# Staging of the output gate z in its own half-sized pool, and a pool of its own for what the attention lays over it, in a hybrid two-layer decoder

## The chip, the cores and the metric

The kernel runs on one core of one Trainium2 chip. The metric is the device time of one execution in microseconds (us); the figure for a kernel is the median over its runs. The engines are TensorE (PE; its weight loads are shown apart as PEld), VectorE (DVE), ScalarE (ACT), GpSimd (POOL) and SyncE (SP), which issues most of the DMAs. Each engine works through its own queue in order. SBUF is the memory on the core, PSUM the accumulators that TensorE writes.

## What is computed

Two layers, each of the form h += RMSNorm(mixer(RMSNorm(h))), then h += sigmoid(h W_g) * (p W_p). The mixer of layer 0 is retention and mLSTM heads, that of layer 1 sixteen attention heads in four groups and an S5 branch. The change lies in layer 1, in the attention and its gate z:

```python
proj = (u @ w_in).astype(F32)
nq, kc, vc, ks, vs, kw, vw, ng, nz, su, sz = _split(proj, CD_SIZES)
y_nsa = nsa(nq, kc, vc, ks, vs, kw, vw, ng, ...)   # compressed, selected and sliding-window branches
y_nsa = y_nsa * jax.nn.silu(nz)
mix = jnp.concatenate([y_nsa, y_s5], -1).astype(u.dtype)
return mix @ w_out
```

Inside `nsa` each token attends to 63 compressed blocks, to 4 selected blocks of 64 keys, and to a window of 512 keys; the three results are added with gates of their own. Everything is float32.

## The kernel before

All matrix products but a few are made of three reduced-precision products: a matrix x is kept as a rounded part `hi` and a remainder `lo`, and hi·hi, hi·lo and lo·hi are added up in PSUM. ACT writes `hi`, DVE (or POOL) the remainder.

The program is written as one long function, `body`. It doesn't fix the order of the instructions: a scheduler with a time model of its own puts them in order on each engine when the program is built, and waits are set from the places that tiles take in SBUF. A tile whose place overlaps an older tile waits until that tile is done with; the scheduler knows of this wait and orders the queues by it. With `reuse_waits="tile"` such a wait is set tile by tile.

Layer 1 first makes its projections (`nsa_projections`, a generator that is advanced one piece at a time, called `gen`). Each piece is a product `pj` into one PSUM bank, ACT and DVE work on it into a staging tile, and a DMA to DRAM. The pieces are 16 of the queries (staging `qst`), 8 of keys (`kst`), 8 of values (`vst`, L1111), and 16 of the gate z (`zt`, L1133): tanh on ACT (L1134), a product on DVE (L1135), a store to `zD` on SP (L1136). All staging tiles have the tag `st` in the pool `pd[0]`; a tile of z uses half of a place of 4,096 bytes per partition. The pool is `pd` first, and `pd2` from L1255 on, three places, on the right-hand side of SBUF, just below the layer's normalised input `vh`, `vl`.

The attention works in 32 units, one group of four heads by one tile of 128 queries (`units`). For a unit, `head` (L1348) makes the compressed branch: scores `cs`, `scc` (L1367 to L1375), the mask `mg` of the selected blocks, and `cp`. `scores` (L1412) makes the other two branches, window (b=1) and selection (b=0): products `sc`, a pass of DVE per piece that adds the mask and finds the maximum (L1425), and the exponential on ACT (L1428) into `pr`; `scale` (L1433) divides by the sum. `values` (L1482) then takes 128 keys at a time: four turns of `pr` on TensorE (`pt`, L1487), the split into `pthh` on ACT (L1478) and `pthl` on DVE (L1479), two products `av`. At the end of the unit `oc` and `ob` collect the result, and it is multiplied by the unit's z, `zn`, which SP loads from `zD` (L1627).

The last z pieces run while the attention begins: the loop at L1451 advances `gen` and puts the heads of units 0 and 1 and both `probabilities` of unit 0 among the last of them. Then `ph3` closes (L1460), the places of `vh` and `vl` come free, and pool `n2` opens (L1469). Its tiles lie on the left, from 144,960 bytes up: `zn` (three of 1,024), `pthh` (three of 2,048, from 148,032), `pthl` (three of 2,048, from 154,176 to 160,320), `oc`, `ob`. `pd2` has 151,520 to 163,808. So the last two `pthh`, all `pthl`, `oc` and `ob` lie on staging places, and `zn` and the first `pthh` don't.

Beside the attention runs `filler`, which advances the S5 branch and the output projection by a credit per unit: its first piece loads `w_glu` (`raw`, split to `whi`, `wlo`, L159 and L160 on ACT and POOL) and two tiles of `y5D` (L1528) that ACT splits to `fhi` (L1499).

Of the kernel before, what the change touches and what calls it, by code (L numbers as in the profile page):

```python
# [17 lines left out]
FT = mybir.dt.float32  # L18
# [79 lines left out]
def body(tc, A, out, dbg=None):  # L98
# [24 lines left out]
    def const_load(p, name, bufs=1):  # L123
        o, n = LAY[name]
        x = p.tile([128, n], FT, name="c_" + name, tag="c_" + name, bufs=bufs)
        nc.scalar.dma_start(x, A["consts"][:, o:o + n])
        return x
# [40 lines left out]
    def chunk(w, segs, nkt=8, kt0=0, gain=None, pack=True):  # L168

        if pack and sum(b for _, b in segs) <= 256:  # L170
            x = [load_w(w, segs, kt0 + 4 * k, 4, gain) for k in range(nkt // 4)]
            return [tuple(y[:, 2 * j:2 * j + 2] for y in c) for c in x for j in range(2)]
        return [load_w(w, segs, kt0 + 2 * k, 2, gain) for k in range(nkt // 2)]
# [668 lines left out]
    class Ext:  # L842
# [5 lines left out]
        def next(self):  # L848
            self.n += 1
            return self.p[self.pat[(self.n - 1) % len(self.pat)]]  # L850
# [228 lines left out]
    def nsa_projections(pd):  # L1079
# [47 lines left out]
        for c in range(4):  # L1127
            ck = chunk(W1, [(2608 + 256 * c, 256)])
            for half in range(2):
                for m in range(2):  # L1130
                    ps = pz[0][0].tile([128, 512], FT, name="pj", tag=pz[0][1])
                    proj_col(ps, uT, half, ck, m * 128)
                    zt = pd[0].tile([128, 2, 512], FT, name="zt", tag="st")[:, 0]  # L1133
                    s.activation(zt, ps, AF.Tanh, scale=0.5)  # L1134
                    v.scalar_tensor_tensor(zt, zt, 1.0, ps, op0=OP.add, op1=OP.mult)  # L1135
                    nc.sync.dma_start(zD[2 * c + m, :, half * 512:(half + 1) * 512], zt)  # L1136
                    yield
# [19 lines left out]
    with ExitStack() as e:  # L1157
        ed = ExitStack()
        pd = [ed.enter_context(tc.tile_pool(name="pd", bufs=3, reuse_waits="tile"))]
# [4 lines left out]
        gen = nsa_projections(pd)  # L1164
# [87 lines left out]
        ed.close()  # L1252
        n1 = ctx.enter_context(tc.tile_pool(name="n1", bufs=1, reuse_waits="tile"))
        nq = ctx.enter_context(tc.tile_pool(name="nq", bufs=3, reuse_waits="tile"))
        pd[0] = e.enter_context(tc.tile_pool(name="pd2", bufs=3, side="right", reuse_waits="tile"))  # L1255
        scaus, wmask = const_load(n1, "scaus"), const_load(n1, "wmask")
        kmask, force = const_load(n1, "kmask"), const_load(n1, "force")
        late = const_load(n1, "late")
# [10 lines left out]
        for kv in range(2):  # L1269
# [55 lines left out]
            else:  # L1325
# [3 lines left out]
                s.activation(vcT[:63, :, 0:64], p3_, AF.Copy)  # L1329
                v.tensor_tensor(vcT[:63, :, 64:128], p3_, vcT[:63, :, 0:64].bitcast(FT), op=OP.subtract)  # L1330
                s.activation(vcT[64:127], vcT[:63].bitcast(FT), AF.Copy)
        for _ in range(9):
            next(gen)
        ec.close()
        px_.close()
        nh = ctx.enter_context(tc.tile_pool(name="nh", bufs=2, reuse_waits="tile"))
# [130 lines left out]
    ext1 = Ext(dict(x=xf), "xxwxwwxw")  # L1467
    with ExitStack() as e:
        n2 = e.enter_context(tc.tile_pool(name="n2", bufs=2, reuse_waits="tile"))  # L1469
        pT = e.enter_context(tc.tile_pool(name="pT", bufs=3, space=PSUM, reuse_waits="tile"))  # L1470
        pV = e.enter_context(tc.tile_pool(name="pV", bufs=1, space=PSUM, reuse_waits="tile"))
        pF = e.enter_context(tc.tile_pool(name="pF", bufs=1, space=PSUM, reuse_waits="tile"))
# [150 lines left out]
        FOFF = -1000  # L1623
        for n, (gg, i) in enumerate(units):
            rows = slice(i * 128, (i + 1) * 128)
            zt = n2.tile([128, 2, 128], FT, name="zn", tag="zn", bufs=3)
            nc.sync.dma_start(zt, zD[2 * gg:2 * gg + 2, :, rows].rearrange("a p k -> p a k"))  # L1627
            if n % 8 == 2 and gg < 3:
                KV[gg + 1] = group(gg + 1)
# [33 lines left out]
            step(gg, ns / 2)  # L1663

            a4 = acc.rearrange("p (a b k) -> p a b k", a=2, b=2)
            oc = n2.tile([128, 2, 128], FT, name="oc", tag="oc", bufs=1)
            ob = n2.tile([128, 2, 128], FT, name="ob", tag="ob", bufs=1)
            lo_, up = slice(0, 64), slice(64, 128)
            for b, here, there in ((0, lo_, up), (1, up, lo_)):
                s.activation(oc[here], a4[there, :, b], AF.Copy)  # L1670
# [74 lines left out]
```

## Time and profile before

| | us |
|---|---|
| median of 3 runs | 2356.01 |
| lowest, highest run | 2354.99, 2358.60 |
| profiled execution | 2355.67 |
| its span, first to last instruction | 2353.6 |
| TensorE busy in the span | 2273.9 |
| DVE, ACT, POOL busy | 1469.6, 1073.4, 487.9 |

The profile gives for each instruction its start, its length, how long its engine had been idle before it, and what ended that idle time. A window row gives the busy time of each engine in a stretch and the TensorE clock that the throttle granted, 1.00 being 2.4 GHz and 0.50 being 1.2. Matmuls overlap, so the time that one costs is read from a run of them, not from its own length.

### The profile page before, as it was taken

To read this page: it belongs to the slowest core of one execution; us is meant where nothing else is said; L and a number is where in the kernel's file an instruction comes from. 1 tells how busy PE (TensorE), PEld (TensorE's weight loads), DVE (VectorE), ACT (ScalarE), POOL (GpSimd) and SP (SyncE) were. 2 spreads that over 40 slices of the span, in tenths; PEclk is the share of its full clock that TensorE was granted. 3 is DMA by queue.
4 is the path that set the end of the run, shared out by engine and by line. 5 is a ranking of instruction groups with operands and counts; after the bars stand their busy time and mean duration, and the time that the engine had idled before them with its cause. 6 is when DMAs were issued, how large, how long until landed. Compare 5 with 4: busy or idle time off the path is not lost.

```text
span 2353.6 us, 34485 instructions
## 1 busy us (share of the span) xinstructions
PE 2273.9 (97%) x11974; PEld 1904.1 (81%) x11974; DVE 1469.6 (62%) x3893; ACT 1073.4 (46%) x2345; POOL 487.9 (21%) x585
## 2 busy tenths in 40 slices
PE   7999999999999999999999999989999989999898
PEld 6888889787888788888888889768988878878677
DVE  6777746755654424444287353368887898888943
ACT  6223323433332432233232233167787786778821
POOL 0222200000000000200000010034354244566720
PEclk9999999999999999999999999989999999999999
DMA  6423312020221645424367524442363443355643
GB/s 160 92 79 107 97 50 72 19 72 27 81 72 37 210 148 206 136 90 136 112 193 246 142 75 131 120 124 77 95 180 107 123 127 97 103 172 155 199 165 111
DMA packets 266696, 279.27 MB, mean 119 GB/s; under 512 B 54384, under 2 KB 200408, under 8 KB 266490
## 3 DMA queue, kind: packets, MB, share of 16 engines
q1 hardware_dynamic: 254810, 244.48, 34.3%
q10 hardware_dynamic: 8096, 23.67, 3.0%
q0 software_dynamic: 3616, 8.92, 1.4%
q8 instruction: 95, 1.56, 0.3%
q14 instruction: 79, 0.65, 0.1%
HBM read 189.84 MB, written 88.42 MB: 118 GB/s over the span
## 4 chain that ended last, share of the span: by engine, by line
PE 82%; DVE 7%; DMA 4%; ACT 2%; SPq 2%; issue 2%; POOL 1%; POOLq 0%; DVEq 0%; ACTq 0%
PE pj L139 41%; PE op L139 8%; PE gp L139 7%; PE fp L139 4%; PE av L139 4%; PE sc L139 4%; PE pt L1487 3%; PE yp L139 2%; PE gl L139 2%; DVE pr L1425 2%; PE trp L214 1%; PE pp L139 1%; PE hp L139 1%; PE kvp L139 1%; PE cs L139 1%
## 5 line engine op out<-in xcount | busy, mean ns | idle before, releaser
L139 PE MATMUL pj<-whi,uh 128*128 128x512 f32 (+2 forms) x768 | 277.9, 363 | 4.5 <-ACT whi L163 2.9
L139 PE MATMUL pj<-wlo,uh 128*128 128x512 f32 (+2 forms) x768 | 277.5, 361 | 0.0
L139 PE MATMUL pj<-whi,ul 128*128 128x512 f32 (+2 forms) x768 | 277.2, 361 | 0.0
L1428 ACT ACTIVATE pr<-pr,nm 128x640 f32<-128x640 f32 (+7 forms) x256 | 187.3, 732 | 65.1 <-DVE nm L1425 62.2
L139 PE MATMUL pj<-vh,whi 128*128 128x512 f32 x512 | 204.4, 400 | 0.2 <-ACT vh L218 0.2
L139 PE MATMUL pj<-vl,whi 128*128 128x512 f32 x512 | 201.9, 394 | 0.0
L139 PE MATMUL pj<-vh,wlo 128*128 128x512 f32 x512 | 201.6, 394 | 0.0
L164 DVE SCALAR_TENSOR_TENSOR wlo<-raw,gnp,whi 128x256 fp32r<-128x256 f32 (+3 forms) x264 | 145.1, 588 | 78.4 <-ACT whi L163 77.3
L1479 DVE TENSOR_TENSOR pthl<-pt,pthh 128x512 fp32r<-128x512 f32 x264 | 177.8, 685 | 15.9 <-ACT pthh L1478 13.8
L163 ACT ACTIVATE whi<-raw,gnp 128x256 fp32r<-128x256 f32 (+3 forms) x264 | 138.0, 585 | 82.4 <-PE pj L139 38.0
L139 PE MATMUL op<-whi,mhl 128*128 128x512 f32 x520 | 165.9, 397 | 2.3 <-ACT mhl L218 1.7
L1487 PE MATMUL pt<-consts,pr 128*128 128x128 f32 x1056 | 162.9, 279 | 5.3 <-DVE pr L1442 2.0
L139 PEld LDWEIGHTS pj<-whi,uh 128*128 128x128 f32 x768 | 144.8, 189 | 27.6 <-ACT whi L163 3.2
L1478 ACT ACTIVATE pthh<-pt 128x512 fp32r<-128x512 f32 x264 | 150.1, 592 | 34.3 <-PE pt L1487 30.2
L139 PEld LDWEIGHTS pj<-wlo,uh 128*128 128x128 f32 x768 | 145.5, 190 | 22.5 <-issue 0.7
L139 PEld LDWEIGHTS pj<-whi,ul 128*128 128x128 f32 x768 | 145.0, 189 | 22.2 <-issue 0.2
L1487 PEld LDWEIGHTS pt<-consts,pr 128*128 128x128 f32 x1056 | 131.9, 144 | 29.6 <-issue 2.9
L139 PE MATMUL sc<-kh,q 128*128 128x320 f32 (+5 forms) x384 | 141.4, 370 | 10.4 <-DVE nm L1425 8.8
L1442 POOL TENSOR_SCALAR pr<-pr,cf 128x640 f32<-128x640 f32 (+4 forms) x64 | 114.9, 1796 | 154.0 <-DVE cf L1437 84.3
L139 PE MATMUL gp<-whi,mhl 128*128 128x512 f32 x448 | 144.5, 397 | 0.3 <-ACT mhl L218 0.3
L139 PE MATMUL sc<-kl,q 82*128 82x320 f32 (+5 forms) x384 | 127.0, 333 | 0.0
L139 PE MATMUL av<-pthl,vt 128*128 128x512 f32 x264 | 115.3, 437 | 7.1 <-DVE pthl L1479 6.5
(452 smaller groups left out, 5557.3 us busy)
## 6 DMA issues: line engine op xcount, KB each, us to landing
raw<-in_ab_w_in_dram SPq DMA_DIRECT2D x100, 256.0 KB
raw<-in_cd_w_in_dram SPq DMA_DIRECT2D x30, 512.0 KB
yD<-fy SPq DMA_DIRECT2D x48, 256.0 KB
raw<-in_ab_w_out_dram SPq DMA_DIRECT2D x16, 512.0 KB
raw<-in_pe_gate_dram SPq DMA_DIRECT2D x16, 512.0 KB
qD<-qst SPq DMA_DIRECT2D x16, 512.0 KB
q<-qD SPq DMA_DIRECT2D x32, 256.0 KB
fin<-yD SPq DMA_DIRECT2D x32, 256.0 KB
```

What stands on the lines that cost most here:

```text
L139: return t.matmul(o, l, r, start=start, stop=stop, **k)
L163: s.activation(hi[:, k], raw[:, k], AF.Copy, scale=gain(kt0 + k))
L164: v.scalar_tensor_tensor(lo[:, k], raw[:, k], gain(kt0 + k), hi[:, k].bitcast(FT), op0=OP.mult, op1=OP.subtract)
L214: t.transpose(ps[:, k * 128:(k + 1) * 128], x[:, (k4 + k) * 128:(k4 + k + 1) * 128], ident)
L1425: v.tensor_tensor_reduce(pr[:, x:y], ps[:, :y - x], mask[:, x:y], op0=OP.add, op1=OP.min, scale=-1.0, scalar=nm[:, 0:1] if c else 3e38, ac ...
L1428: s.activation(pr[:, :nk], pr[:, :nk], AF.Exp, scale=-1.0, bias=nm[:, c:c + 1], accum_out=sums[:, b, h:h + 1])
L1442: (v if eng == "v" else g).tensor_scalar(P[h][:, :nk], P[h][:, :nk], cf[:, h:h + 1], None, op0=OP.mult)
L1478: s.activation(hi[:dst_shape], ps[:dst_shape], AF.Copy)
L1479: v.tensor_tensor(lo[:dst_shape], ps[:dst_shape], hi[:dst_shape].bitcast(FT), op=OP.subtract)
L1487: t.transpose(ps[:, h * 128:(h + 1) * 128], P[h][:, k * 128:(k + 1) * 128], ident)
```

## The change

The z pieces get a tag `zt` of their own with tiles of 2,048 bytes. After the eight pieces of values `pd2` is closed and `pd3` opened at the same right-hand end, with three places of 2,048 bytes: 157,664 to 163,808. `zn`, `oc` and `ob` move from `n2` to a new pool `n3` behind it. `n2` now begins with `pthh` (144,960 to 151,104), then `pthl` (to 157,248), and nothing of it lies on a place of `zt`; `zn`, `oc` and `ob` (157,248 to 162,368) do.

```diff
--- before.py
+++ after.py
@@ -1130,7 +1130,7 @@
                 for m in range(2):
                     ps = pz[0][0].tile([128, 512], FT, name="pj", tag=pz[0][1])
                     proj_col(ps, uT, half, ck, m * 128)
-                    zt = pd[0].tile([128, 2, 512], FT, name="zt", tag="st")[:, 0]
+                    zt = pd[0].tile([128, 512], FT, name="zt", tag="zt")
                     s.activation(zt, ps, AF.Tanh, scale=0.5)
                     v.scalar_tensor_tensor(zt, zt, 1.0, ps, op0=OP.add, op1=OP.mult)
                     nc.sync.dma_start(zD[2 * c + m, :, half * 512:(half + 1) * 512], zt)
@@ -1252,7 +1252,8 @@
         ed.close()
         n1 = ctx.enter_context(tc.tile_pool(name="n1", bufs=1, reuse_waits="tile"))
         nq = ctx.enter_context(tc.tile_pool(name="nq", bufs=3, reuse_waits="tile"))
-        pd[0] = e.enter_context(tc.tile_pool(name="pd2", bufs=3, side="right", reuse_waits="tile"))
+        ev = ExitStack()
+        pd[0] = ev.enter_context(tc.tile_pool(name="pd2", bufs=3, side="right", reuse_waits="tile"))
         scaus, wmask = const_load(n1, "scaus"), const_load(n1, "wmask")
         kmask, force = const_load(n1, "kmask"), const_load(n1, "force")
         late = const_load(n1, "late")
@@ -1329,8 +1330,11 @@
                 s.activation(vcT[:63, :, 0:64], p3_, AF.Copy)
                 v.tensor_tensor(vcT[:63, :, 64:128], p3_, vcT[:63, :, 0:64].bitcast(FT), op=OP.subtract)
                 s.activation(vcT[64:127], vcT[:63].bitcast(FT), AF.Copy)
-        for _ in range(9):
+        for _ in range(8):
             next(gen)
+        ev.close()
+        pd[0] = e.enter_context(tc.tile_pool(name="pd3", bufs=3, side="right", reuse_waits="tile"))
+        next(gen)
         ec.close()
         px_.close()
         nh = ctx.enter_context(tc.tile_pool(name="nh", bufs=2, reuse_waits="tile"))
@@ -1467,6 +1471,7 @@
     ext1 = Ext(dict(x=xf), "xxwxwwxw")
     with ExitStack() as e:
         n2 = e.enter_context(tc.tile_pool(name="n2", bufs=2, reuse_waits="tile"))
+        n3 = e.enter_context(tc.tile_pool(name="n3", bufs=1, reuse_waits="tile"))
         pT = e.enter_context(tc.tile_pool(name="pT", bufs=3, space=PSUM, reuse_waits="tile"))
         pV = e.enter_context(tc.tile_pool(name="pV", bufs=1, space=PSUM, reuse_waits="tile"))
         pF = e.enter_context(tc.tile_pool(name="pF", bufs=1, space=PSUM, reuse_waits="tile"))
@@ -1623,7 +1628,7 @@
         FOFF = -1000
         for n, (gg, i) in enumerate(units):
             rows = slice(i * 128, (i + 1) * 128)
-            zt = n2.tile([128, 2, 128], FT, name="zn", tag="zn", bufs=3)
+            zt = n3.tile([128, 2, 128], FT, name="zn", tag="zn", bufs=3)
             nc.sync.dma_start(zt, zD[2 * gg:2 * gg + 2, :, rows].rearrange("a p k -> p a k"))
             if n % 8 == 2 and gg < 3:
                 KV[gg + 1] = group(gg + 1)
@@ -1663,8 +1668,8 @@
             step(gg, ns / 2)
 
             a4 = acc.rearrange("p (a b k) -> p a b k", a=2, b=2)
-            oc = n2.tile([128, 2, 128], FT, name="oc", tag="oc", bufs=1)
-            ob = n2.tile([128, 2, 128], FT, name="ob", tag="ob", bufs=1)
+            oc = n3.tile([128, 2, 128], FT, name="oc", tag="oc", bufs=1)
+            ob = n3.tile([128, 2, 128], FT, name="ob", tag="ob", bufs=1)
             lo_, up = slice(0, 64), slice(64, 128)
             for b, here, there in ((0, lo_, up), (1, up, lo_)):
                 s.activation(oc[here], a4[there, :, b], AF.Copy)
```

The instructions are the same ones. On TensorE, DVE, ACT and SP their order is unchanged up to the selected branch of unit 0 and moved from there on. In the following rows `pthh`, `pthl`, `pt` with the lowest numbers are those of unit 0's window branch; the next five to eight are its selected branch.

ACT, around the exponentials (L1428, now L1432) of the selected branch of unit 0, before:

```order
L1440 ACTIVATE pr_13848<-pr_13848,cf_13870 128x1024
L1134 ACTIVATE zt_13902<-pj_13877 128x512
L159 ACTIVATE whi_13989<-raw_13988 128x1024
L159 ACTIVATE whi_13995<-raw_13994 128x1024
L1370 ACTIVATE scc_14198<-scc_14198 128x4x48
L1499 ACTIVATE fhi_14012<-fin_14014 128x4x128
L1499 ACTIVATE fhi_14012<-fin_14018 128x4x128
L1478 ACTIVATE pthh_13938<-pt_13933 128x512
L1478 ACTIVATE pthh_13949<-pt_13944 128x512
L1478 ACTIVATE pthh_13960<-pt_13955 128x512
```

and now:

```order
L1134 ACTIVATE zt_13826<-pj_13801 128x512
L1483 ACTIVATE pthh_13945<-pt_13940 128x512
L1483 ACTIVATE pthh_13956<-pt_13951 128x512
L1483 ACTIVATE pthh_13967<-pt_13962 128x512
L1432 ACTIVATE pr_13830,sums_13749<-pr_13830,nm_13831 128x1024
L1483 ACTIVATE pthh_13978<-pt_13973 128x512
L1483 ACTIVATE pthh_13989<-pt_13984 128x512
L1432 ACTIVATE pr_13841,sums_13749<-pr_13841,nm_13842 128x1024
L1432 ACTIVATE pr_13852,sums_13749<-pr_13852,nm_13853 128x1024
L1432 ACTIVATE pr_13863,sums_13749<-pr_13863,nm_13864 128x1024
L1444 ACTIVATE pr_13852<-pr_13852,cf_13874 128x1024
L1134 ACTIVATE zt_13906<-pj_13881 128x512
```

The five `pthh` of the window branch stood behind the last z piece, two `whi`, the next unit's `scc` and two `fhi`; now they stand among the exponentials. The two `fhi` now have three `pthh` of the selected branch ahead of them, and the fourth stands behind the first `fhi`.

On TensorE, accordingly, the ten `av` and the last eight `pt` of the window branch stand now between the selected branch's `sc`. Between the last piece of `pj` and the first `av` that needs a `pthh` from behind `fhi` stood two pairs of `sc` and eight `cs`; now it is seven pairs of `sc`, eight `cs`, twenty `pt` and six `av`.

DVE, after the scaling of unit 0's selected branch, before:

```order
L1135 SCALAR_TENSOR_TENSOR zt_13902<-zt_13902,pj_13877 128x512
L1367 TENSOR_TENSOR scc_14198<-cs_14189,c_kmask_12062 128x4x48
L1368 TENSOR_REDUCE m4_14199<-scc_14198 128x4
L1369 TENSOR_TENSOR scc_14198<-scc_14198,m4_14199 128x4x48
L1371 TENSOR_REDUCE m4_14199<-scc_14198 128x4
L1372 RECIPROCAL m4_14199<-m4_14199 128x4
L1375 TENSOR_TENSOR scc_14198<-scc_14198,m4_14199 128x4x48
L1381 TENSOR_REDUCE ph_14208<-scc_14198 128x48
```

and now:

```order
L1135 SCALAR_TENSOR_TENSOR zt_13906<-zt_13906,pj_13881 128x512
L1371 TENSOR_TENSOR scc_14205<-cs_14196,c_kmask_12062 128x4x48
L1429 ISA pr_14242,nm_14243<-sc_14248,c_wmask_12060,nm_14243 128x320
L1429 ISA nm_14243 128x1
L1372 TENSOR_REDUCE m4_14206<-scc_14205 128x4
L1373 TENSOR_TENSOR scc_14205<-scc_14205,m4_14206 128x4x48
L1429 ISA pr_14253,nm_14254<-sc_14255,c_wmask_12060 128x320
L1429 ISA nm_14254 128x1
L1484 TENSOR_TENSOR pthl_14067<-pt_14061,pthh_14066 128x512
```

The compressed branch of the next unit (`scc`) stood alone there; now passes of scores and `pthl` lie between its steps.

SP, from the last z store on, before:

```order
L1136 DMA zD_92<-zt_13902 128x512
L1533 DMA fin_14022<-z5D_10091 128x256
L1533 DMA fin_14142<-z5D_10091 128x256
L155 DMA raw_14000<-in_s5_w_glu_dram 128x2x512
L1627 DMA zn_13929<-zD_92 128x2x128
L1627 DMA zn_14182<-zD_92 128x2x128
L1627 DMA zn_14681<-zD_92 128x2x128
L155 DMA raw_14006<-in_s5_w_glu_dram 128x2x512
```

and now:

```order
L1136 DMA zD_92<-zt_13906 128x512
L1538 DMA fin_14029<-z5D_10091 128x256
L1538 DMA fin_14149<-z5D_10091 128x256
L155 DMA raw_14007<-in_s5_w_glu_dram 128x2x512
L1632 DMA zn_13936<-zD_92 128x2x128
L1632 DMA zn_14189<-zD_92 128x2x128
L1632 DMA zn_14688<-zD_92 128x2x128
L155 DMA raw_14013<-in_s5_w_glu_dram 128x2x512
```

The order is the same; the first `zn` load, whose place now lies on z staging, has a wait for the store at the top as a new one. Behind it stands the fourth load of `w_glu`.

## Rows read from the trace of the kernel before

**Rows 1.** The page, busy time, share of the span and instructions of an engine

```profile
PE 2273.9 (97%) x11974; PEld 1904.1 (81%) x11974; DVE 1469.6 (62%) x3893; ACT 1073.4 (46%) x2345; POOL 487.9 (21%) x585
```

**Rows 2.** Waits of TensorE, 1560 to 2250 us: total, times, longest

```profile
PE av L139 <- ACT pthh L1478: 8.1, 2, 7.8
```

**Rows 3.** Windows: length, then busy us of each engine, granted clock, DMA share

```profile
1480.00:1500.00 20.00, 20.00 (x93) 16.50 (x93) 4.83 (x10) 2.79 (x5) 0.00 (x0) 1.00 0.53 139
1552.50:1556.00 3.50, 0.00 (x0) 0.00 (x0) 2.91 (x5) 0.89 (x2) 3.50 (x2) 0.73 1.19 259
1556.00:1560.20 4.20, 0.00 (x0) 0.00 (x0) 3.89 (x10) 1.76 (x4) 2.79 (x4) 0.50 1.16 330
1560.20:1562.00 1.80, 1.76 (x6) 1.42 (x7) 1.80 (x4) 1.14 (x3) 1.80 (x4) 0.50 1.09 348
1562.00:1564.00 2.00, 2.00 (x8) 1.60 (x8) 0.71 (x2) 1.74 (x3) 1.70 (x4) 0.50 1.08 351
1600.00:2250.00 650.00, 612.83 (x3511) 515.04 (x3510) 550.61 (x1649) 503.67 (x1115) 334.14 (x334) 0.97 0.43 133
```

**Rows 4.** Timeline, TensorE, ACT, SP and DVE near the gap: start, length, idle before

```profile
1550.34 0.31 PE L139 MATMUL sc<-kh,q 128*128 128x320 f32 x1
1550.63 0.19 PE L139 MATMUL cs<-kcH,q 128*128 128x48 f32 x1
1551.33 0.27 PE L139 MATMUL cs<-kcL,q 82*128 82x48 f32 x1
1560.24 0.79 PE L139 MATMUL av<-pthh,vt 128*128 128x512 f32 x1 [7.77 <-ACT pthh L1478]
1530.09 0.83 ACT L1428 ACTIVATE pr<-pr,nm 128x640 f32<-128x640 f32 x1 [0.29 <-DVE nm L1425]
1530.83 0.19 ACT L1428 ACTIVATION_READ_ACCUMULATOR pr<-pr,nm 128x1 f32 x1
1558.25 0.63 ACT L1499 ACTIVATE fhi<-fin 128x512 fp32r<-128x512 f32 x1 [3.07 <-DMA fin<-y5D]
1559.60 1.55 ACT L1478 ACTIVATE pthh<-pt 128x512 fp32r<-128x512 f32 x3
1564.52 1.06 ACT L159 ACTIVATE whi<-raw 128x1024 fp32r<-128x1024 f32 x1 [0.29 <-DMA raw<-in_s_w_glu_dram]
1551.37 3.08 SPq L1528 DMA_DIRECT2D fin<-y5D  x2
1554.55 0.78 SPq L1136 DMA_DIRECT2D zD<-zt  x1
1559.11 0.37 SPq L155 DMA_DIRECT2D raw<-in_s_w_glu_dram  x1
1560.21 1.89 DVE L1479 TENSOR_TENSOR pthl<-pt,pthh 128x512 fp32r<-128x512 f32 x3
```

**Rows 5.** Chain of waits, 1520 to 1600 us: start, length, what

```profile
1538.23 1.31 PE pt L1487 x12
1544.86 5.66 PE pj L139 x24
```

**Rows 6.** Groups by form, 1537.5 to 1546 us, and the tile pthl (min/median/max ns)

```profile
L1425 DVE CUSTOM_DVE_ANT_0 pr<-sc,mg,nm 128x512 f32<-128x512 f32 x4 | 3.0, 750 | 1.1 <-PE sc L139 1.1
L1425 DVE CUSTOM_DVE_ANT_0 pr<-sc,mg 128x512 f32<-128x512 f32 x4 | 2.8, 688 | 4.9 <-PE sc L139 4.9
L1479 DVE TENSOR_TENSOR pthl<-pt,pthh x264: 648/685/693, 1560.2 to 2244.5; 128x512 fp32r<-128x512 f32 x132
```

**Rows 7.** Groups by form, 1550.5 to 1560.5 us, and line L1369 (min/median/max ns)

```profile
L160 POOL TENSOR_TENSOR wlo<-raw,whi 128x1024 fp32r<-128x1024 f32 x2 | 4.8, 2402 | 1.3 <-ACT whi L159 1.3
L1369 DVE TENSOR_TENSOR scc<-scc,m 128x192 f32<-128x192 f32 x1 | 2.2, 2179 | 0.0
L1375 DVE TENSOR_TENSOR scc<-scc,m 128x192 f32<-128x192 f32 x1 | 1.3, 1330 | 0.0
L1369 DVE TENSOR_TENSOR scc<-scc,m x32: 183/326/2179, 1471.1 to 2194.3; 128x256 f32<-128x256 f32 x4, 128x224 f32<-128x224 f32 x4, 128x192 f32<-128x192 f32 x4, 128x160 f32<-128x160 f32 x4
```

## The prediction

> **What bounds the kernel now.** I read the page first: TensorE is busy for 2273.9 us [rows 1], 97% of the span, so an edit helps only if it closes one of TensorE's few gaps. The profiled execution took 2355.67 us, 0.34 us under the median of the three runs, 2356.01 us. The waits of TensorE come next: in the whole attention the longest single one is 7.8 us of the group in which the value product `av` waits for ACT's rounded turned probabilities `pthh` [rows 2]. The windows then show where and how: between 1552.5 and 1560.2 us TensorE does nothing at all, the granted clock falls to 0.50, and it stays at 0.50 until 1564, so that the 1.76 + 2.00 us of work after the gap run at 1.2 instead of 2.4 GHz [rows 3]. The timeline says why ACT is late: `pthh` is a job of 0.6 us, but it stands in ACT's in-order queue behind `fhi`, which waits until 1558.25 for a load of y5D that SP issued only at 1551.37 [rows 4]. The probabilities themselves were ready long before: their twelve turns on TensorE stand at 1538.23 us [rows 5]. So the scheduler put `pthh` late because its place was taken by the staging of z, and what it was put behind made it later still.
>
> **The change, part by part.**
>
> *Projections.* The z staging keeps three buffers and the same activations, products and stores; only their size and place differ. TensorE has no gap there, and the first tiles wait for stores of `vst` that are no younger than before. Cost 0; the cover is slack on both engines: from 1480 to 1500 us TensorE is busy all the time, DVE for 4.8 us and ACT for 2.8 [rows 3]. Without it a late staging tile would stop the projection that waits for its PSUM bank.
>
> *`pthh` and `pthl` of the first window branch move ahead*, between the eight score passes of the selected branch of unit 0. That brings 3.2 us of TensorE work forward: ten `av` matmuls at 5.66/24 = 0.236 us and eight turns at 1.31/12 = 0.109 us [rows 5]. It costs time there, because DVE sets the pace of these scores: eight passes of 0.75 and 0.69 us, with 1.1 us of idle between them [rows 6]. Five `pthl` of 0.685 us [rows 6] add 3.4 us. If they fill all idle time the phase grows by 2.3 us, if none by 3.4. I take 2.7, since an instruction that waits for ACT rarely fits the gap whole. The projection that follows and the loads that SP issues behind the last score and the last projection move by the same 2.7.
>
> *After that projection.* Before, TensorE went from 1550.34 to 1560.24 us, 9.9 us, on two score pairs of 0.29 us and eight `cs` in 0.8 us [rows 4], 1.4 us of work: 8.5 us lost. Now it starts there at 1553.0 and has more in front of it: seven score pairs (2.0), eight `cs` (0.8), twenty turns (2.2) and six `av` (1.4), 6.4 us. Then it needs a `pthh` that again stands behind `fhi` in ACT's queue. The load lands 2.7 later, at 1560.95; `fhi` takes 0.63, the exponential ahead of `pthh` 0.83 and 0.19, and the first of three `pthh` that take 1.55 some 0.6 [rows 4]: 1563.2. From 1553.0 that is 10.2 us for 6.4 of work, so 3.8 us are lost where 8.5 were. This is the new wait; what is queued behind it on ACT are the next `pthh` and exponentials, on TensorE everything. Bounds: 0, if the loads come sooner, since they then share the DMA with less; 8.5, as long as the old one.
>
> *Clock.* Before, 3.76 us of busy time at half clock cost 1.9 us [rows 3]. With a gap of half the length I take 0.6, between 0 and 1.9.
>
> *The rest of the attention* has the same instructions in another order for most of its first units, the same order for about a fifth of its length in the middle, and again at the end. It leaves 37 us of 650 without TensorE work [rows 3]; if a tenth of that comes or goes, 3.7 us either way. This is an estimate, and I take 0. The work on DVE that lay under the old gap has to go beside TensorE now; DVE has room for it.
>
> *Sum against the profiled execution:* -8.5 + 3.8 (gap), -3.2 + 2.7 (scores), -1.9 + 0.6 (clock) = -6.5 us: 2349.2, and with the median's 0.34 above it **2349.5 us**.
>
> **A rule against the change.** In the old gap a subtraction on DVE with both inputs in SBUF took 2.18 us where the same line's median is 0.326; it ended when the first 2.4 us remainder on POOL, begun just before it, was over, and another of its kind took 1.33 [rows 7]. The Trainium skill (SBUF — State Buffer, Who interferes with whom) says that a DVE instruction with two SBUF inputs contends with a GpSimd instruction that reads SBUF, and that the one that starts first has the shared port pair for its whole length. By that rule the trace agrees. Before, nothing of TensorE's hung on those two. In the new order the subtraction stands in DVE's queue ahead of scores and of `pthl` that TensorE waits for, and falls in the same POOL work.
>
> **The rivals.**
>
> *B, DVE held up behind POOL.* For: the rows just named, and the new DVE order. Against: the new wait for `fhi` may cover it. If both come on top in full, 2.4 + 1.3 = 3.7 us: 2353.2. Chance 0.14.
>
> *C, the wait only moves.* `fhi` still stands ahead of a `pthh`. If TensorE loses as much there as it did (8.5, so 4.7 more than I take) and the clock falls as long (1.3 more), 2355.5. Against: 6.4 us of work now stand ahead of it. That the change does nothing at all is excluded, as the order of the built program shows `pthh` ahead. Chance 0.13.
>
> *D, slower: the z loads.* The loads `zn` now go where the staging was, so in SP's queue the first waits until the last z store has landed. That store was issued at 1554.55, and its landing is bounded by the reader of its place, which started at 1560.21: up to 5.7 us. Behind it stands the fourth load of the GLU weights; before, that took from 1559.11 to 1564.52 until ACT's `whi` began, 5.4 us [rows 4]. If ACT has to sit through both, in front of exponentials and `pthh`, 11.1 us, and TensorE pays another 1.9 for its clock: 2362.5. It decides from where that `whi` starts later than about 1567, when TensorE has used up what is ready. Against: SP was busy with other loads for most of that time anyway, and ACT comes to this `whi` only after four more `pthh`. Chance 0.10.
>
> *E, more.* No new gap (3.8 and 0.6 less): 2345.1. Chance 0.08.
>
> **How the numbers follow.** The forecast itself has 0.55, with a range of its own of 2346 to 2352 from the bounds of the score phase, the gap and the reordered rest. The range of 2345 to 2357 takes in B and C as well and leaves out D, most of E and the tails, some 0.2. A difference of 0.2%, 4.7 us, is about what a measurement of this kernel can tell from none, so faster means under 2351.3: the forecast but for 0.07 of it, and E, 0.56. Same: that 0.07, B and C, 0.34. Slower: D, 0.10.
>
> **What would show it.** Right: no wait of `av` for `pthh` of over 4 us near the start of the attention; the first `pthh` near 1539 us instead of 1559.6; the last score of the selected branch of unit 0 some 2.7 us later; `fhi` waiting for y5D until about 1561; a stretch at 0.50 after it of under 2 us; and from there every landmark earlier by 6 to 7 us up to the end. Wrong: an idle TensorE from 1556 to over 1564, or an ACT `whi` waiting for its weights past 1567 (D), DVE subtractions of 2 us with scores waiting behind them (B), or a lead of 6 us at 1570 that is gone by 2250, which would put the fault on the reordered rest.

## The result and the profile after

The changed kernel takes 2366.49 us (median of 6 runs, 2362.47 to 2377.81) where the kernel before takes 2353.01 (6 runs, 2348.4 to 2358.6): ratio 1.006, 95% interval 1.0043 to 1.0077, some 13 us slower. A second series gave 2361.44 and a ratio of 1.0039 (1.0025 to 1.0053). The prediction was 2349.5 with a range of 2345 to 2357: the time lies outside the range, and it moved the other way. The two series of the same kernel differ by 5 us, so differences between kernels of different series are uncertain by about that much. One execution of the q-first kernel below took 3240.52 us at a granted clock of 0.641; its ratio leaves it out.

The profiled execution took 2371.7 us, its span is 2369.8, and TensorE is busy for longer than before [rows 1]. The page of the changed kernel, busy time of the engines:

```profile
PE 2285.5 (96%) x11974; PEld 1912.5 (81%) x11974; DVE 1469.3 (62%) x3893; ACT 1073.3 (45%) x2345; POOL 490.6 (21%) x585
```

The same number of matmuls is busy 11.6 us longer, which already points to the clock. The timeline of the changed kernel near the old gap, first ACT, then SP, TensorE and DVE (start, length, idle before; the columns of [rows 4]; SPq is SP's DMA queue):

```profile
1537.75 1.57 ACT L1483 ACTIVATE pthh<-pt 128x512 fp32r<-128x512 f32 x3 [0.74 <-PE pt L1492]
1559.82 0.63 ACT L1504 ACTIVATE fhi<-fin 128x512 fp32r<-128x512 f32 x1 [3.63 <-DMA fin<-y5D]
1561.16 0.58 ACT L1483 ACTIVATE pthh<-pt 128x512 fp32r<-128x512 f32 x1
1563.93 1.06 ACT L159 ACTIVATE whi<-raw 128x1024 fp32r<-128x1024 f32 x1
1567.66 1.06 ACT L159 ACTIVATE whi<-raw 128x1024 fp32r<-128x1024 f32 x1 [1.38 <-DMA raw<-in_s_w_glu_dram]
1558.42 0.39 SPq L155 DMA_DIRECT2D raw<-in_s_w_glu_dram  x1
1561.34 1.40 SPq L1632 DMA_DIRECT2D zn<-zD  x3
1562.83 0.41 SPq L155 DMA_DIRECT2D raw<-in_s_w_glu_dram  x1
1573.91 0.37 SPq L1357 DMA_DIRECT2D q<-qD  x1
1561.79 0.50 PE L139 MATMUL av<-pthh,vt 128*128 128x512 f32 x1 [1.99 <-ACT pthh L1483]
1564.37 0.47 PE L139 MATMUL sc<-kh,q 128*128 128x448 f32 x1 [0.34 <-DVE nm L1429]
1578.38 0.40 PE L139 MATMUL cs<-kcH,q 128*128 128x40 f32 x1 [1.38 <-DMA q<-qD]
1562.38 1.47 DVE L1379 TENSOR_TENSOR scc<-scc,m 128x192 f32<-128x192 f32 x1
```

Up to 1562 us it goes as forecast: the first `pthh` starts at 1537.75 instead of 1559.60, the wait of `av` that was 7.77 us [rows 4] is 1.99. Then at 1578 TensorE waits for the `q` of the fourth unit. Before, the same `cs` stood 12 us later in TensorE's queue, without a wait, and the clock was at 1.00:

```profile
1590.96 0.18 PE L139 MATMUL cs<-kcH,q 128*128 128x40 f32 x1
1575.00:1580.00 5.00, 5.00 (x31) 4.30 (x30) 4.71 (x14) 3.89 (x8) 2.40 (x2) 1.00 0.27 80
1580.00:1585.00 5.00, 5.00 (x40) 4.85 (x39) 2.82 (x9) 3.57 (x9) 1.11 (x2) 1.00 0.11 31
```

The windows of the changed kernel (columns of [rows 3]):

```profile
1552.50:1556.00 3.50, 2.37 (x19) 2.01 (x18) 3.34 (x9) 3.50 (x8) 3.20 (x2) 1.00 1.15 247
1556.00:1560.20 4.20, 3.76 (x23) 2.94 (x23) 3.72 (x13) 0.57 (x2) 1.64 (x1) 1.00 1.13 307
1560.20:1562.00 1.80, 0.21 (x1) 0.21 (x2) 0.23 (x1) 1.80 (x5) 1.27 (x1) 1.00 0.80 296
1562.00:1564.00 2.00, 2.00 (x12) 1.58 (x11) 2.00 (x3) 2.00 (x6) 1.37 (x2) 1.00 0.69 201
1575.00:1580.00 5.00, 3.49 (x20) 2.77 (x18) 4.26 (x14) 3.90 (x9) 1.42 (x2) 0.84 0.57 166
1580.00:1585.00 5.00, 5.00 (x17) 4.32 (x18) 4.18 (x11) 2.24 (x4) 2.99 (x1) 0.50 0.39 110
1600.00:2250.00 650.00, 608.80 (x3460) 511.92 (x3458) 540.50 (x1622) 494.64 (x1097) 329.31 (x327) 0.96 0.43 130
```

Where the clock was 0.50 it is now 1.00 to 1564. But from 1578 to 1585 it is at 0.50, after a wait of only 1.38 us, and from 1600 to 2250 us TensorE is idle for 41.2 us instead of 37.2 [rows 3] and the mean clock is 0.96 instead of 0.97. TensorE's waits in the attention of the changed kernel, 1560 to 2250 us (total, times, longest; [rows 2] is its line of before):

```profile
PE av L139 <- DVE pthl L1484: 9.8, 8, 3.0
PE sc L139 <- DVE nm L1429: 9.5, 15, 2.1
PE cs L139 <- DMA q<-qD: 6.6, 7, 1.4
PE av L139 <- ACT pthh L1483: 3.0, 3, 2.0
```

The old wait is gone from the list and nothing of its size has come in its place.

**Where the gain went.** All 2612 matmuls `cs`, `sc`, `av`, `gl` and `fp` (the last two are products of `filler`) from 1500 us on are in every trace. Weighed by their columns they give a measure of how far TensorE has come, and so the time at which an execution has done what the kernel before had done at 1535 us, at 1573 us, and at its last `av` (2245.24 us). The table has, for each profiled execution, the difference in us to the kernel before: at 1535 us, before the change does anything; what comes on top to 1573 us; from there to the last `av`; and from the last `av` to the end of the span. The runs below the second line are the experiments.

| run | at 1535 | to 1573 | rest of the attention | gate stage | span |
|---|---|---|---|---|---|
| changed kernel | -0.9 | -7.1 | +17.4 | +6.8 | +16.2 |
| changed kernel again | -3.8 | -6.9 | +11.4 | +4.1 | +4.8 |
| staging only | -0.9 | -0.4 | +0.8 | +0.1 | -0.3 |
| n3 only | -2.9 | +0.7 | +0.9 | -0.5 | -1.8 |
| q first | -1.5 | -5.8 | -2.9 | +6.1 | -4.1 |
| hold | -3.4 | -6.7 | -2.8 | +2.6 | -10.3 |
| tail | -1.2 | -5.6 | +12.8 | -2.0 | +4.0 |
| cs later | -2.3 | -6.2 | +7.3 | 0.0 | -1.2 |
| q first, tail | -0.2 | -6.0 | +2.5 | +4.4 | +0.8 |
| POOL behind | -0.9 | -7.1 | +11.1 | +2.4 | +5.5 |
| hold, tail | +1.1 | -7.1 | -0.7 | +2.2 | -4.5 |
| before, reordered | -3.6 | -0.7 | +9.6 | -0.1 | +5.1 |
| hold, reordered | -2.1 | -7.6 | +6.4 | +2.5 | -0.8 |

The first column is wander of the stages before: n3 only, which changes nothing there, strays by 2.9 us. The second says that the forecast gain is there, in the changed kernel and wherever `pthh` goes ahead of `fhi`: 5.6 to 7.6 us, where the prediction had 6.5. The third and fourth say that it is lost again, and more, behind 1573 us. Single executions of one order differ by up to 6 us in the third column.

The measure leaves out the turns `pt`. With each of them counted as 237 columns (0.109 us against 0.236 for a product of 512, [rows 5]) the gain to 1573 us is 7.0 to 8.6 us in the ten runs with `pthh` ahead, and the third column grows by 0.4 to 1.7. A cut inside a reordered stretch is uncertain by about that much.

Where the two orders part and meet tells more. On TensorE, DVE and ACT the changed kernel has the order of the kernel before again from 1895 to about 2078 us (times of the kernel before). Its three executions, the third being the run called tail, lose 12.0, 8.1 and 8.6 us from 1573 to 1895; in the stretch of equal order they lose nothing (-0.2, -3.7, -0.5); from 2078 to the last `av` they lose 5.6, 7.0 and 4.8. Two places repeat almost exactly: 7.5, 7.2 and 7.4 us are lost from 1800 to 1820, and 5.5, 3.8 and 3.9 from 2078 to 2160, where staging only and n3 only, which have the order of the kernel before throughout, stay within 0.1. Two other runs come back to that order earlier, cs later from 1890 to 2212 us and q first from 1981 to the end of the attention, and there they lose nothing (-1.8 and -0.8). The two runs staging only and n3 only show how far one order strays by itself: +2.0 and -2.5, -3.0 and -1.4, +1.8 and +4.8 in the three stretches.

### The profile page after: what moved, and what is told of

Its sections match the earlier page's. It is cut to its first block, busy times and chain, and to the rows that moved or that the text cites. A ratio compares the mean times of both kernels' runs of the same rounds, so it can differ in the third digit from the quotient of the medians.

```text
span 2369.8 us, 34486 instructions
## 1 busy us (share of the span) xinstructions
PE 2285.5 (96%) x11974; PEld 1912.5 (81%) x11974; DVE 1469.3 (62%) x3893; ACT 1073.3 (45%) x2345; POOL 490.6 (21%) x585
## 4 chain that ended last, share of the span: by engine, by line
PE 85%; DVE 5%; DMA 4%; issue 2%; ACT 1%; SPq 1%; POOL 1%; ACTq 0%; DVEq 0%; POOLq 0%
PE pj L139 42%; PE op L139 7%; PE gp L139 7%; PE fp L139 5%; PE av L139 4%; PE sc L139 4%; PE pt L1492 4%; PE yp L139 2%; PE gl L139 2%; PE trp L214 1%; DVE pr L1429 1%; PE cs L139 1%; PE pp L139 1%; PE hp L139 1%; PE kvp L139 1%
## 5 line engine op out<-in xcount | busy, mean ns | idle before, releaser
L1432 ACT ACTIVATE pr<-pr,nm 128x640 f32<-128x640 f32 (+7 forms) x256 | 187.1, 731 | 62.6 <-DVE nm L1429 58.8
L139 PE MATMUL sc<-kh,q 128*128 128x320 f32 (+5 forms) x384 | 143.5, 376 | 12.3 <-DVE nm L1429 11.6
```

Source lines behind the costliest of these rows:

```text
L139: return t.matmul(o, l, r, start=start, stop=stop, **k)
L1432: s.activation(pr[:, :nk], pr[:, :nk], AF.Exp, scale=-1.0, bias=nm[:, c:c + 1], accum_out=sums[:, b, h:h + 1])
```

## The experiments

Three theories were on the table. **O**: the loss comes from the new order of the rest, which the scheduler chose because the first units came out differently. **P**: it comes from the new places, `zn`, `oc` and `ob` over the staging, rival D of the prediction. **B**: DVE held up behind POOL, rival B. An edge of issue order, in the diffs below, says only that one instruction stands behind another in the queue of their engine; it adds no wait and changes no place or data.

```
def behind(x, y):
    tc.add_manual_dep(x.ins, y.ins.name, mybir.DependencyInfo(
        mybir.DependencyClass.NoSync, mybir.DependencyReason.DATA), reason="order")
```

**Staging only.** The kernel before with

```diff
-zt = pd[0].tile([128, 2, 512], FT, name="zt", tag="st")[:, 0]
+zt = pd[0].tile([128, 512], FT, name="zt", tag="zt")
...
+ev.close(); pd[0] = e.enter_context(tc.tile_pool(name="pd3", bufs=3, side="right", reuse_waits="tile"))
```

> Only the staging half of the change: z tiles of half the size, the last two of them in the pool of their own; zn, oc and ob stay where they were. Every engine keeps the order of the kernel before. Theory O (the loss comes from the new order that both halves together bring, not from the places): the time of the kernel before, 2353 within 3 us, with the 7.8-us wait of av for pthh at 1552 us still there. Theory P (the new places cost): a part of the 13.5 us could show here, 2356 to 2366.

2353.78 us, ratio 1.0001 (0.9988 to 1.0014).

**n3 only.** The kernel before with

```diff
+n3 = e.enter_context(tc.tile_pool(name="n3", bufs=1, reuse_waits="tile"))
-zt = n2.tile([128, 2, 128], FT, name="zn", tag="zn", bufs=3)
+zt = n3.tile([128, 2, 128], FT, name="zn", tag="zn", bufs=3)
```

and the same for `oc` and `ob`.

> Only the other half: zn, oc and ob in a pool of their own behind the turned probabilities, so that they lie over the old, full-size staging. Every engine keeps the order of the kernel before. Theory P (the loads of z and what oc and ob wait for, rival D of the prediction): slower, up to 2366, with the first zn load or the ACT whi behind it late. Theory O: 2353 within 3 us, and the 7.8-us wait at 1552 us still there.

2353.51 us, ratio 1.0005 (0.9995 to 1.0014). Either half alone leaves the order of every engine as it was, and the old wait with it. TensorE's waits, 1540 to 1570 us, staging only:

```profile
PE av L139 <- ACT pthh L1478: 7.8, 1, 7.8
```

and n3 only:

```profile
PE av L139 <- ACT pthh L1478: 8.0, 1, 8.0
```

So the halves move the order together or not at all: with the staging alone two `pthl` still lie on it, with `n3` alone all three do. And the places cost nothing by themselves: in n3 only `zn` lies on the full-size staging, its first load is issued at 1556.59, 3.3 us behind the load ahead of it (0.4 us in the kernel before), and the time is the same. P and D don't explain the loss; hold, below, has all places of the change and shows it once more.

**q first.** The changed kernel; `qld` holds the last `q` load of each unit.

```diff
-load_w(w, [(hf * 512, 512)], kt0 + 2 * k, 2, wp=xf)
+load_w(w, [(hf * 512, 512)], kt0 + 2 * k, 2, wp=xf); kt0 == 8 and behind(last_load[0], qld[3])
```

> The changed kernel, with one edge of issue order added: the four loads of the second output weight are issued behind the q loads of the fourth unit, where the changed kernel has them ahead. Theory O, in its narrow form (the lead goes at 1577 us, where cs waits for that q and the clock falls): no wait of cs for q there, TensorE 8 us ahead of the kernel before at 1600 instead of 2.5, and the end 5 to 6 us earlier, 2361, if the rest keeps its losses; the rest gets another order once more, so that 2350 to 2370 is open. Theory P: no difference, 2366.

2354.67 us, ratio 1.0003 (0.9992 to 1.0014): 12 us less than the changed kernel (7 less than its second series), more than the narrow theory gave, and not by its way. The `q` was issued no earlier, at 1574.55, and `cs` still waited, 0.70 and 0.52 us; what differs from the first execution of the changed kernel is that the clock stayed up. Windows of this run:

```profile
1575.00:1580.00 5.00, 3.65 (x25) 2.93 (x24) 4.40 (x12) 3.10 (x7) 1.40 (x2) 1.00 0.70 220
1580.00:1585.00 5.00, 5.00 (x34) 4.61 (x34) 4.83 (x13) 3.05 (x6) 2.59 (x2) 1.00 0.65 211
```

The edge changed the order behind it up to about 1981 us, from where on it is that of the kernel before up to the gate stage, and the rest of the attention, +17.4 in the changed kernel, is -2.9 here. That is O in its wide form, not in the narrow one.

**Hold.** The changed kernel with every `pthh` behind the last tanh of the z staging, `lastz`, on ACT:

```diff
-s.activation(hi[:dst_shape], ps[:dst_shape], AF.Copy)
+behind(s.activation(hi[:dst_shape], ps[:dst_shape], AF.Copy), lastz[0])
```

> The changed kernel, with one edge of issue order added: every pthh is issued on ACT behind the last tanh of the z staging, so that no pthh goes among the selected scores of unit 0, but five of them still go ahead of fhi. Theory O: the long wait at 1552 stays closed, TensorE is 8 to 10 us ahead at 1573 as in the changed kernel, and what is left of it at the end differs from the changed kernel's loss since the later order differs: anywhere from 2345 to 2365. Theory P: 2366, as the places are those of the changed kernel. If the pthh among the scores are what costs (more waits on DVE), 2349.

2346.04 us, ratio 0.9971 (0.996 to 0.9981). ACT in this run:

```profile
1547.20 0.60 ACT L1134 ACTIVATE zt<-pj 128x512 f32<-128x512 f32 x1 [1.95 <-PE pj L139]
1547.69 1.57 ACT L1483 ACTIVATE pthh<-pt 128x512 fp32r<-128x512 f32 x3
1554.93 0.63 ACT L1504 ACTIVATE fhi<-fin 128x512 fp32r<-128x512 f32 x1 [1.11 <-DMA fin<-y5D]
```

Five `pthh` go behind the last z piece and ahead of `fhi`. The places are those of the changed kernel, the gain to 1573 us is the same (6.7), and here it stays. From soon after the eighteenth unit's head (1867 us) every engine has the order of the kernel before again, the start of the gate stage too. This fall back was not foreseen, as the expectation left 2345 to 2365 open. Up to there its order is neither that of the kernel before nor that of the changed kernel, and it loses nothing either. The window over the attention:

```profile
1600.00:2250.00 650.00, 611.79 (x3493) 511.19 (x3493) 550.28 (x1633) 498.60 (x1105) 331.86 (x329) 0.98 0.45 137
```

This is the version that beats both kernels, by 0.3% against the kernel before.

**The changed kernel again,** beside the next three.

> The changed kernel once more, beside the next three. Theory O, as it stands after four runs (the loss is in the new order: first at 1577 us, where cs of the fourth unit waits 1.4 us for a q issued at 1573.9 and the clock then stays at 0.50 until 1585; then in more such stretches; at last at the start of the gate stage): the same places lose again, with the time at 2363 to 2372. If the half clock after 1577 us is an accident of that one execution, TensorE keeps most of its 8 us of lead at 1590 here, and the time is nearer to 2360.

2361.44 us. The wait of `cs` is at its place, but what it costs differs from execution to execution. TensorE in this run, and its windows:

```profile
1575.27 0.29 PE L139 MATMUL cs<-kcH,q 128*128 128x40 f32 x1 [1.13 <-DMA q<-qD]
```

```profile
1575.00:1580.00 5.00, 4.73 (x32) 4.35 (x33) 4.71 (x13) 3.46 (x8) 4.08 (x3) 1.00 0.37 109
1580.00:1585.00 5.00, 5.00 (x41) 4.71 (x39) 4.83 (x18) 2.64 (x6) 1.88 (x4) 1.00 0.11 33
```

The wait is 1.13 instead of 1.38 us and the clock does not fall. In the run tail, which has the same order up to the gate stage, the wait is 1.00 us and the clock falls (0.95 from 1575 to 1580, 0.71 from 1580 to 1585). The rest of the attention still loses 11.4 us here: there are many such places, and which of them pulls the clock down changes from one execution to the next.

**Tail.** At its start the last gate stage (the layer's second step, sigmoid(h W_g) * (p W_p), with products `gp`) of the changed kernel has twenty turns `trp` of three `h` tiles in a row, ahead of 72 `gp`; the kernel before has 19 `gp`, whose data are there, between the first tile's eight turns and the second's. The prediction, which looked at the order of the attention alone, overlooked this. In this run the third tile is turned later, and the first tile's second product goes ahead of the second tile's first:

```diff
-T[i + 2] = front(order[i + 2]); proj(order[i], 0, T[i]); proj(order[i + 1], 0, T[i + 1]); proj(order[i], 1, T[i])
+proj(order[i], 0, T[i]); proj(order[i], 1, T[i]); proj(order[i + 1], 0, T[i + 1]); T[i + 2] = front(order[i + 2])
```

for the first pair of tiles only.

> The changed kernel with only the first steps of the last gate stage in another order: the transposes trp of the third tile, which wait for a load of h, stand behind the products that are ready, where the changed kernel has them ahead. Up to there every engine keeps the changed kernel's order. Theory O: the two waits of trp for h of 5.5 us in all shrink to 2 or less and the half clock behind them goes: 4 to 7 us less than the changed kernel, 2360 to 2362. If the load of h is late because POOL's last products are, and not the order: no difference.

2359.37 us, ratio 1.0028 (1.0014 to 1.0041), beside 1.0039 (1.0025 to 1.0053) for the changed kernel in the same series. Waits of TensorE at that place, the changed kernel:

```profile
PE trp L214 <- DMA h<-hD: 5.5, 2, 4.8
```

and tail:

```profile
PE trp L214 <- DMA h<-hD: 0.4, 1, 0.4
```

The wait goes as expected, and the gate stage is 6 to 9 us shorter by the table. The median fell by only 2, and the intervals overlap: the wait and its cause are shown, its worth in the time is not settled.

**cs later.** The changed kernel; `avm[15]` is the product of the third window block of unit 1.

```diff
 for h in range(4):
-    mm(ps[:, h * 64:h * 64 + w], q2[:, h, :], kcH[:, gg, :w], True, False)
+    x = mm(ps[:, h * 64:h * 64 + w], q2[:, h, :], kcH[:, gg, :w], True, False)
+    if (gg, i) == units[3] and h == 0: behind(x, avm[15])
```

> The changed kernel with one edge of issue order added: the first cs of the fourth unit is issued behind the first seven av of unit 1, where the changed kernel has it ahead of them. TensorE keeps the changed kernel's order but for these rows until about 1775 us, and another one in some stretches after that; the start of the gate stage falls back to the order of the kernel before. Theory O: no wait of cs at 1577, the clock stays at 1.00 to 1590, TensorE is 7 to 8 us ahead of the kernel before at 1600 instead of 1 to 2; with the gate stage's order 4 to 7 more at the end: 2352 to 2358. If the loss of the lead at 1577 has another cause (DVE, the turned probabilities): under 2 us ahead at 1600, 2360 to 2366.

2358.5 us, ratio 1.0025 (1.0013 to 1.0036): just above what was expected. The wait is gone and the clock is 1.00 from 1575 to 1590, and TensorE is 5.9 us ahead of the kernel before at 1600, where the changed kernel was 0.9 ahead (7.0 in the second execution). The order of the changed kernel held for longer than the expectation says, to about 1827 us, and lost 5 us by 1620 and 6 more between 1800 and 1820 as in every trace of that order.

**q first, tail.** The q-first kernel with the tail edit.

> The kernel of the q-first edge (which ran at 2354.7 and lost some 6 us at the start of the gate stage, with a wait of trp for h of 6.5 us) with the gate stage started in the order of the run before this one. Every engine keeps the q-first order up to there. Theory O: the wait shrinks to 2 us or less and the time falls by 4 to 6 us to 2349 to 2351. If the load of h sets the pace there: no difference.

2350.7 us, ratio 0.9996 (0.9984 to 1.0008). The time is where it was expected, but not for the reason: `trp` still waits for `h`,

```profile
PE trp L214 <- DMA h<-hD: 4.9, 1, 4.9
```

where the q-first kernel waited 6.5. Here the loads of `h` stand in SP's queue behind the last stores of `filler`, and they set the pace. Whether the difference of 4 us is more than the wander of two series stays open.

**POOL behind.** The cs-later kernel, with the third of four remainders `wlo` behind the scaling `pr` that followed it on POOL (`prg[26]`):

```diff
-x = g.tensor_tensor(lo, raw, hi.bitcast(FT), op=OP.subtract)
+x = g.tensor_tensor(lo, raw, hi.bitcast(FT), op=OP.subtract); behind(x, prg[26])
```

> The kernel of the cs edge (2358.5), with one more edge of issue order on POOL: the remainder wlo of the third weight load in the middle of the attention is issued behind the scaling pr of 640 columns, where all traces of the changed order have it ahead. Only some 18 rows of the program move. In four traces of that order the small product cf on DVE took 1.3 us longer than usual there, until that wlo was over, a wait of sc for nm of 2.1 us followed at about 1812 us, and TensorE lost 5 to 7 us between 1800 and 1820. Theory B (rival B of the prediction at another place: DVE held up behind POOL): that wait shrinks to under 1 us, TensorE loses 1 to 3 us there, and the time is 3 to 5 us less, 2354 to 2355. If the wait is one of DVE's own order: no difference.

2361.43 us, ratio 1.0036 (1.0024 to 1.0048): no gain. DVE's small product and the `sc` that waits, in the cs-later kernel:

```profile
1812.69 1.48 DVE L1441 TENSOR_TENSOR cf<-cf,gts 128x4 f32<-128x4 f32 x1
1815.53 0.44 PE L139 MATMUL sc<-kh,q 128*128 128x384 f32 x1 [2.09 <-DVE nm L1429]
```

and with POOL behind:

```profile
1813.20 0.16 DVE L1441 TENSOR_TENSOR cf<-cf,gts 128x4 f32<-128x4 f32 x1
1814.73 0.44 PE L139 MATMUL sc<-kh,q 128*128 128x384 f32 x1 [0.78 <-DVE nm L1429]
```

The mechanism of B is as it was thought: without the POOL remainder beside it `cf` takes 0.16 us instead of 1.48, and the wait falls from 2.09 to 0.78. The Trainium skill's rule on the shared port pair (SBUF — State Buffer, Who interferes with whom) agrees with that. TensorE's loss between 1800 and 1820 us went from 6.2 to 4.7, about what the wait gave back; the clock fell there all the same (0.66 from 1815 to 1820, 0.69 without the edge). Between 1880 and 1900, where the two kernels have one order, this execution lost 7 us and the other 2. So the stall is worth 1 to 2 us at its place, and the time of the kernel, which strays by more, does not show it.

**Hold, tail.**

> The kernel that holds pthh behind the z staging (2346.0) with the gate stage started as in the run on the tail: the third tile's transposes behind the products that are ready. Every engine keeps the order up to there. If the start of the gate stage still costs: the wait of trp for h of 2.9 us shrinks, 2343 to 2345. If the load of h sets the pace: 2346.

2350.17 us, ratio 0.9982 (0.9972 to 0.9992), above both figures that were expected. The wait of `trp` is 3.0 us where it was 2.9: there too the load of `h` sets the pace, and the edit is not worth having. With the run before it this is a second measurement of one order of the attention: faster than the kernel before in both, by 2 to 7 us.

**Before, reordered.** The kernel before, its places, its gap; each unit's first `cs` from the fourth unit on stands behind the third window product of the unit two earlier (`avm` by unit).

```diff
+    if units.index((gg, i)) > 2 and h == 0: behind(x, avm[2 * units.index((gg, i)) - 4])
```

> The kernel before, with the places of before, and an edge of issue order for every unit from the fourth on: its first cs stands behind the third pair of window products of the unit two earlier. Every engine keeps the order of before up to about 1645 us, so the 7.8-us wait at 1552 is there; from there the rest of the attention is scheduled in another order, and the gate stage starts as in the changed kernel. Theory O (the rest of the attention is worth some 10 us either way, whatever the first units do): TensorE level with before at 1640, and a difference of 3 to 10 us by the end, more likely a loss, since the gate stage's start alone costs 4 to 7: 2355 to 2364. If a new order as such costs nothing and the change's places or its first units make the rest slow: 2353.

2360.79 us, ratio 1.0034 (1.0022 to 1.0046). Nothing moves up to 1643 us, the old wait is there,

```profile
PE av L139 <- ACT pthh L1478: 7.8, 1, 7.8
```

and the new order of the rest costs 9.6 us of attention. Its window:

```profile
1600.00:2250.00 650.00, 610.85 (x3460) 513.08 (x3458) 546.57 (x1633) 498.78 (x1102) 332.69 (x329) 0.96 0.44 132
```

Against [rows 3] TensorE is idle for 2 us more, and the clock is 0.96 instead of 0.97.

**Hold, reordered.** The same edges in the hold kernel.

> The same edges in the kernel that holds pthh (2346.0): the gain of 8 to 10 us at 1573 us stays, and the rest gets another order than before's. Theory O: a part or all of the gain is lost again, 2347 to 2360. If a new order as such costs nothing: 2346.

2356.07 us, ratio 1.002 (1.0009 to 1.0031): 10 us more than hold and 6 more than hold, tail, though the gain to 1573 us is there in full (7.6). These two show that a change of the rest's order alone can cost as much as was lost: 8 us with the places and the first units of the kernel before, 6 to 10 with those of the change. They do not show that every new order costs: q first and hold have others and lose nothing. And the order that they test is not the changed kernel's own; for that one the evidence is the stretches where it departs from the order of before and comes back to it.

## Why the prediction was wrong

*What bounds the kernel* was read rightly: the gap, `fhi` in front of `pthh`, the place as its cause.

*Projections, cost 0*: right, by staging only (1.0001).

*Scores, +2.7*: the five `pthl` went among the passes, 3.4 us by their lengths. The first `sc` of this phase started at 1536.21 instead of 1537.60 and the projection behind it at 1545.47 instead of 1544.86 [rows 5], so the phase grew by 2.0 us, less than the lower bound of 2.3: the next pass starts 0.61 us after a `pthl`, not 0.685.

*The gap, 3.8 instead of 8.5*: right in its mechanism and nearly in size. `fhi` again stood in front of a `pthh`; TensorE waited 1.99 us for it and 1.13 for DVE before that, 3.1 in all. The projection ended at 1551.13, not 1553.0.

*Clock, 0.6*: 1.00 throughout in the first execution, 1.4 us lost in q first (0.83 from 1560 to 1570, 8.0 us of work). Of the seven executions with this order four show 0.83 there and three 1.00.

*Their sum, -6.5*: the seven executions with the changed kernel's order of these units have -5.6 to -7.1, mean -6.4, and with the turns counted -7.0 to -8.6, mean -7.9. So the mechanism held and gave what was forecast or somewhat more; that one of the means meets the sum to a tenth is luck.

**The step that failed** is *the rest of the attention*: "if a tenth of that comes or goes, 3.7 us either way. This is an estimate, and I take 0." The runs show +17.4, +11.4 and +12.8 for that order. Two things were wrong with it. The base was the idle time alone and left out the clock. Counted over equal work, from 1573 us to the last `av`, TensorE is idle for 37.2 us before and for 5.9, 5.2 and 6.2 more in the three executions of the changed order; half its busy time at a granted clock of 0.50, which is what the half clock costs, is 16.2 us before and 11.1, 3.7 and 3.4 more. Together that is 17.0 of 17.4, 8.9 of 11.4 and 9.6 of 12.8. In before, reordered, 2.1 of idle and 8.4 of half clock stand against 9.6. And a tenth was a guess: of the other orders of the rest that ran, three (the changed kernel's, and the two reordered runs) cost 6 to 17 us more than the order of the kernel before, and two (q first, hold) about nothing.

**A term left out** is the start of the gate stage, +6.8 and +4.1: the prediction has nothing for it, and the order there is another.

*Rival B*: there in the row at 1562.38 (1.47 us), but behind the wait for `fhi`, not under it; the scores behind it made TensorE wait 0.34 us at 1564.37, a tenth of B's price. Its other place, at 1812 us, was not looked for. *C*: no, 1.99 us. *D*, the only case given for slower: its wait came, its cost did not. The first `zn` was issued at 1561.34 instead of 1556.83, 4.5 us later, and the fourth GLU load behind it at 1562.83 instead of 1559.11. The `whi` of that load started at 1567.66, after 1.38 us of waiting, past the 1567 that D names (the `whi` at 1563.93 is that of the third load, issued at 1558.42). But TensorE has no wait between 1564.37 and 1578.38. *E*: no, a wait was left. The sign that the prediction named for a fault of the reordered rest, a lead at 1570 that is gone by 2250, is what came; it had been given no chance of its own.

What stays open is which waits of the changed order make up the 11 to 17 us. The stretches that lose are known (1573 to 1600 us with 7.1, 3.6 and 4.5, 1800 to 1820, and 2078 to 2160), but only two of their waits were taken away one by one, at 1577 and at 1812 us, and the medians gave 3 us and nothing.

## What to carry to other kernels

Where a scheduler orders the program, a change of a place is a change of all that comes after: compare the two orders to the very end, and price the part that is only reordered by reordering it alone, without the change. Here that price, 6 to 10 us in the two reordered runs and 11 to 17 in the changed kernel, was larger than the gain of 6 to 8. If the wanted piece can be moved so that the rest keeps an order that loses nothing, the gain is kept: 2346.04 us with an edge of issue order on each `pthh`. That these edges would lead back to the old order was not foreseen.

## What the runs showed of the hardware

A short wait of TensorE cost anything from its own length to several times that. At one and the same place a wait of 1.38 us was followed by 0.50 of the clock until 1585, one of 1.13 us in the next execution by 1.00, and one of 1.00 us in the run tail by 0.50 again. At 1560 us seven executions have the same order and wait 1.95 to 2.19 us; behind it the clock fell to 0.50 in four and stayed at 1.00 in three, with a wait of 1.99 us on either side. The changed kernel's row and its window at 1.00 stand above; in cs later:

```profile
1560.36 0.50 PE L139 MATMUL av<-pthh,vt 128*128 128x512 f32 x1 [1.99 <-ACT pthh L1483]
1560.00:1570.00 10.00, 9.64 (x53) 8.81 (x54) 9.04 (x27) 8.27 (x16) 8.13 (x7) 0.83 0.57 179
```

So the price of a small wait in a busy stretch can't be read from its length. And a stall of DVE behind POOL, 1.3 us on an instruction of 0.16, can be taken away by one position in POOL's queue; TensorE's loss at that place fell from 6.2 to 4.7 us, and the time of the kernel did not show it.
